# Splitting streamed weights into two rounded parts by DMA instead of by ScalarE and VectorE

## The chip, the cores and the metric

The kernel runs on one core of one Trainium2 chip. The metric is the device time of one execution in microseconds. Engines are PE (TensorE), ACT (ScalarE), DVE (VectorE), POOL (GpSimd) and SP (SyncE). A hardware profile of one execution gives the rows below.

## The reference

One layer of a hybrid decoder trunk, 512 tokens, width 1024, everything in float32:

```python
h = rmsnorm(x, g_mix[l])
u = h @ w_in[l]
c_q, c_kv, k_r, u_pool, z, xbc, dt, lru_g, lru_x, gates = jnp.split(u, pts, axis=-1)
...
gates = jax.nn.sigmoid(gates.reshape(b, s, N_BRANCH, D_MODEL))
merged = (gates[:, :, 0] * (y_a @ w_branch[l, 0])
          + gates[:, :, 1] * (y_b @ w_branch[l, 1])
          + gates[:, :, 2] * (y_c @ w_branch[l, 2])
          + gates[:, :, 3] * (y_d @ w_branch[l, 3]))
x = x + merged @ w_out[l]
h2 = rmsnorm(x, g_mlp[l])
x = x + jnp.square(jax.nn.relu(h2 @ w_ff1[l])) @ w_ff2[l]
ple_gate = jax.nn.sigmoid(rmsnorm(x, g_ple[l]) @ w_ple_gate[l])
x = x + (p[l] @ w_ple[l]) * ple_gate
```

The four branches are attention (y_a), causal pooling (y_b), a state-space mixer (y_c) and a gated linear recurrence (y_d). A final norm follows.

## The kernel before, in words

All large products run on PE in a rounded 32-bit format (float32r), with each operand split into a high part (the value rounded to that format) and a low part (the remainder). A product is three matmuls per 128 rows of depth: high by high, high by low, low by high (`mm3`, lines 208 to 210).

The weights are streamed from one tensor W in *units* of 128 partitions by up to 1024 values, 512 KB each. The list UNITS at the top of the file fixes their order. `unit(key)` (line 200) hands out a unit and loads ahead until two units beyond it are requested (LOOK = 2). `load_next` (line 165) loads one: SP's queue brings it into a raw tile (tag wr, two buffers, line 176), ACT copies it into the high part wh, which rounds it (line 177), and DVE subtracts, which gives the low part wl (line 178). wh and wl have three buffers each. Throughout this text a *pair* is one wh with its wl. The next unit takes a pair when PE has read it for the last time.

The stages that matter here, with their units:

- *Branches.* For branch n and column block j, `gate(n, j)` (line 425) multiplies a gate unit by the normed input: 8 depth blocks, 24 matmuls, and a tanh on ACT. `project(n, j)` (line 430) multiplies half a br unit by the branch's output, 12 matmuls; DVE multiplies by the gate and POOL adds to the merged sum (line 439). Branch 2 is interleaved with the projections of the recurrence (lx, lg) and of pooling (pool); branches 3 and 1 follow by themselves.
- *out.* Eight units, 24 matmuls each (line 841).
- *MLP.* Four chunks. In each, eight ff1 units of 24 matmuls (line 919), then 14 *T units* of the second matrix, which is multiplied by a Strassen-Winograd scheme of seven products (`product`, line 881). The T units use the same wh and wl buffers, filled by `right_operand` (line 185) from b tiles that SP loads (line 899) and that POOL subtracts from one another, eight operations per chunk (lines 903 and 904).

A scheduler orders each engine's instructions when the program is built, and each engine then runs its own in order. `tc.high_priority()` puts the loads forward.

Of the kernel before, what the change touches and what calls it, by code (L numbers as in the profile page):

```python
# [10 lines left out]
F32 = mybir.dt.float32  # L11
F32R = mybir.dt.float32r
I32 = mybir.dt.int32
AF = mybir.ActivationFunctionType
ALU = mybir.AluOpType
AX = mybir.AxisListType

P = 128
# [34 lines left out]
UNITS = []  # L53
UIDX = {}
# [72 lines left out]
def trunk(tc, xT, pT, pos, par_d, cst_d, gfin, wblk_d, wpool_d, W, out, dbg=None):  # L127
    nc = tc.nc
    act, dve, pool, pe, sync = nc.scalar, nc.vector, nc.gpsimd, nc.tensor, nc.sync
    TAGS = {"G1": 16, "G2": 16, "G3": 16, "T1": 6, "T2": 8, "T3": 6, "Z": 4, "X": 8}  # L130
    BANKS = {"m": 3, "s": 2, "t": 2, "o": 1}
    with ExitStack() as ctx:
        cp = ctx.enter_context(tc.tile_pool(name="cp", bufs=1))
        ap_ = ctx.enter_context(tc.tile_pool(name="ap", bufs=1))
        wp = ctx.enter_context(tc.tile_pool(name="wp", bufs=1))
# [5 lines left out]
        def nm(s):  # L141
            cnt[0] += 1
            return f"{s}_{cnt[0]}"

        def A(tag, dt=F32, n="a"):
            return ap_.tile([P, S], dt, name=nm(n), tag=tag, bufs=TAGS[tag])
# [18 lines left out]
        def load_next():  # L165
            u = state[0]
            state[0] += 1
            n = UNITS[u][1]
            if UNITS[u][0][0] == "T":
                loaded[u] = right_operand(*UNITS[u][0][1:])  # L170
                return
            with tc.high_priority():
                raw = wp.tile([P, 1024], F32, name=nm("wr"), tag="wr", bufs=2)
                hi = wp.tile([P, 1024], F32R, name=nm("wh"), tag="wh", bufs=3)
                lo = wp.tile([P, 1024], F32R, name=nm("wl"), tag="wl", bufs=3)
                sync.dma_start(out=raw[:, :n], in_=W[u, :, :n])
                act.copy(out=hi[:, :n], in_=raw[:, :n])  # L177
                dve.tensor_tensor(out=lo[:, :n], in0=raw[:, :n], in1=hi[:, :n].bitcast(F32), op=ALU.subtract)  # L178
            loaded[u] = (hi, lo)


# [3 lines left out]
        def right_operand(ch, name, v):  # L185
            hi = wp.tile([P, 1024], F32R, name=nm("wh"), tag="wh", bufs=3)
            lo = wp.tile([P, 1024], F32R, name=nm("wl"), tag="wl", bufs=3)
            with tc.high_priority():
                for u in range(2):
                    kp, c = 2 * v + u, slice(u * S, (u + 1) * S)  # L190
                    src = ff2_raw[ch, {"t2": "b11", "t3": "b12", "t4": "b21"}.get(name, name), kp]
                    act.copy(out=hi[:, c], in_=src)  # L192
                    dve.tensor_tensor(out=lo[:, c], in0=src, in1=hi[:, c].bitcast(F32), op=ALU.subtract)  # L193
                    if name == "b11":
                        dve.tensor_tensor(out=src, in0=ff2_raw[ch, "b22", kp], in1=ff2_raw[ch, "t1", kp], op=ALU.subtract)
                    elif name == "b21":
                        dve.tensor_tensor(out=src, in0=src, in1=ff2_raw[ch, "b11", kp], op=ALU.subtract)
            return hi, lo

        def unit(*key):  # L200
            u = UIDX[key]
            while state[0] <= min(u + LOOK, NRING - 1):
                load_next()
            return loaded.pop(u)
# [16 lines left out]
        def pc(name, i=0, w=1):  # L221
            o, _ = PAR[name]
            return par[:, o + i:o + i + w]
# [93 lines left out]
        for k in range(KD):  # L317
            if k:
                sync.dma_start(out=xres[k], in_=xT[:, k, :])
            if k < 3:  # L320
                load_next()
            if k == 2:
                sync.dma_start(out=cst, in_=cst_d)
            xg.append(split_scaled(xres[k], pc("gmix", k), "G1", "xg"))
            q = A("T3", F32, "sq")
            act.activation(out=q, in_=xres[k], func=AF.Square)
            if acc is None:
                acc = q
            else:
                dve.tensor_tensor(out=acc, in0=acc, in1=q, op=ALU.add)  # L330
        for k in range(KD):
            if k == 5:
                with tc.high_priority():
                    vx = SM(NT, "vx")
                    dve.tensor_scalar(out=vx, in0=token_sums(acc), scalar1=1.0 / D, scalar2=EPS,
                                      op0=ALU.mult, op1=ALU.add)
                    rxb = bcast_tokens(rsqrt(vx, NT), "T1")
            w = loaded.pop(UIDX[("lat", k)])
            for i in range(5):
                c = slice(i * P, (i + 1) * P)  # L340
                mm3(lat_ps[i], w[0][:, c], w[1][:, c], xg[k][0], xg[k][1], k == 0, k == KD - 1)
            if k + 3 < KD:
                load_next()
# [7 lines left out]
        for k in range(KD):  # L351
            n = A("T3", F32, "hn")
# [118 lines left out]
        for t in range(NT):  # L471
# [3 lines left out]
                          in1=pc("dtb", 0, 8).unsqueeze(1).to_broadcast([P, NT, 8]), op=ALU.add)  # L475
# [75 lines left out]
        for hd in range(H):  # L551
# [11 lines left out]
            for kt in range(NT):  # L563
                pt = PS("t")
                n = S - kt * P
# [22 lines left out]
            else:  # L588
# [11 lines left out]
                                 in1=ah.unsqueeze(1).to_broadcast([P, NT, 8]), op0=ALU.mult, op1=ALU.mult)  # L600
# [18 lines left out]
        def bc8(v, n=8):  # L619
            return v.unsqueeze(2).to_broadcast([v.shape[0], n, 64])  # L620
# [4 lines left out]
        def csl(c):  # L625
            return slice(c * P, (c + 1) * P)
# [19 lines left out]
        for g in range(2):  # L646
            ps = PS("s")
            gs = slice(g * 64, g * 64 + 64)
            for c in range(NT):
                pe.matmul(ps[:, csl(c)], lhsT=xbc[4][gs, csl(c)], rhs=xbc[5][gs, csl(c)], start=True, stop=True)  # L650
            dve.tensor_tensor(out=heads(cbm[g], P), in0=heads(ps, P), in1=U.unsqueeze(1).to_broadcast([P, NT, P]),
                              op=ALU.mult)
        gate(0, 6, "G1")
        for c in range(NT):
            for g in range(2):
# [4 lines left out]
                for j in range(4):  # L660
# [4 lines left out]
                                   in1=cbm[g][:, csl(c)].unsqueeze(1).to_broadcast([P, 4, P]), op=ALU.mult)  # L665
# [4 lines left out]
        for c in range(NT - 1):  # L670
# [5 lines left out]
            for g in range(2):  # L676
# [4 lines left out]
                else:  # L681
                    dve.tensor_tensor(out=heads(Rn[gs, 0:256]), in0=heads(R[c][gs, 0:256]),
                                      in1=bc8(etot[gs, c * 8 + g * 4:c * 8 + g * 4 + 4], 4), op=ALU.mult)
# [3 lines left out]
        for c in range(NT):  # L687
# [7 lines left out]
            if c > 0:  # L695
                for g in range(2):
# [5 lines left out]
                                      in1=bc8(eacs[:, c * 8 + g * 4:c * 8 + g * 4 + 4], 4), op=ALU.mult)  # L702
# [93 lines left out]
        for i in range(4):  # L796
            w = unit("pool", i)
            ps = proj(w, hh, KD)
            u = A("T3", F32, "pu")
            act.copy(out=u, in_=ps)  # L800
            src = u
            n = 1
# [148 lines left out]
        for hf in range(2):  # L951
            ws = []
            for k in range(KD):
                raw = A("T1", F32, "pgw")
# [11 lines left out]
        for hf in range(2):  # L966

            for j in range(0, KD, 2):
                ps = PS("t")
                for u in range(2):  # L970
                    for t in range(2):
                        k = j + u
                        pe.transpose(out=ps[:, (2 * u + t) * P:(2 * u + t + 1) * P],
                                     in_=xt[2 * hf + t][k // 4][:, (k % 4) * P:(k % 4 + 1) * P], identity=ident)
# [28 lines left out]
        for hf in range(2):  # L1003
            ws = pgs[hf]
            for t in range(NT):
# [6 lines left out]
                for q in range(nf):  # L1012
# [3 lines left out]
                    for k in range(KD):  # L1016
# [9 lines left out]
                                                          in1=gf[:, hf, c], op=ALU.mult)  # L1026
# [146 lines left out]
```

## Time and profile before

| | |
|---|---|
| median of 3 runs | 981.22 us (980.24 to 982.66) |
| the profiled execution | 982.21 us, its span 980.4 us |
| PE, DVE, ACT, POOL busy | 954.9, 661.4, 489.4, 138.8 us |
| mean granted clock of PE | 0.997 of full speed |
| moved by DMA | 96.95 MB, 99 GB/s |

Busy time is the union of an engine's instructions. Matmuls overlap, so their pitch is read from start to start and not from a row's duration. In a timeline row the bracket says how long the engine was idle before the instruction and what ended that. Names are tiles, out<-in, with buffer numbers left out.

### The profile page before, as it was taken

What the parts mean: (1) busy time and instruction counts of PE and PEld (TensorE: products, weight loads), DVE (VectorE), ACT (ScalarE), POOL (GpSimd) and SP (SyncE); (2) the same over time, 40 slices, a digit from 0 to 9 for tenths busy, and PEclk for the clock granted to TensorE, in tenths of its full rate; (3) what the DMA queues carried; (4) which work ended last, traced back from release to release, by engine and by line L of the source; (5) the groups of instructions that cost most, each with busy time, mean ns of one, the idle gap of its engine ahead of it and who ended that gap; (6) DMA issues with size and microseconds to landing.
All of it is one profiled execution on the core that took longest, in us unless ns stands there. A gap on an engine that the chain in (4) does not pass through costs nothing.

```text
span 980.4 us, 12002 instructions
## 1 busy us (share of the span) xinstructions
PE 954.9 (97%) x4389; PEld 782.4 (80%) x4389; DVE 661.4 (67%) x1156; ACT 489.4 (50%) x860; POOL 138.8 (14%) x107
## 2 busy tenths in 40 slices
PE   7999999999999999999999999999999999999996
PEld 5877788877777887788888888788887888887785
DVE  7768787557885753443433656996897789689636
ACT  6755777768276333222332435543543453456633
POOL 0000000005102423311122001350013005000021
PEclk9999999999999999999999999999999999999998
DMA  5423221214112332332324326134133304424002
GB/s 201 136 76 103 78 74 65 66 44 151 65 65 86 119 108 84 108 108 87 129 86 151 108 76 226 65 129 150 65 101 126 108 31 142 139 81 134 1 1 86
DMA packets 36473, 96.95 MB, mean 99 GB/s; under 512 B 4768, under 2 KB 4800, under 8 KB 36416
## 3 DMA queue, kind: packets, MB, share of 16 engines
q1 hardware_dynamic: 35472, 95.35, 29.5%
q10 hardware_dynamic: 944, 0.85, 0.3%
q8 instruction: 34, 0.56, 0.2%
q14 instruction: 23, 0.19, 0.1%
HBM read 94.01 MB, written 2.18 MB: 98 GB/s over the span
## 4 chain that ended last, share of the span: by engine, by line
PE 81%; DVE 13%; ACT 2%; issue 2%; DMA 2%; ACTq 0%; DVEq 0%
PE psm L208 21%; PE psm L210 21%; PE psm L209 21%; DVE wl L193 4%; PE pss L208 3%; PE pss L209 3%; PE pss L210 3%; DVE xtok L894 2%; DVE wl L178 1%; PE pst L567 1%; PE pst L209 1%; PE pst L208 1%; PE pso L210 1%; PE pso L208 1%; PE pso L692 1%
## 5 line engine op out<-in xcount | busy, mean ns | idle before, releaser
L177 ACT CAST wh<-wr 128x1024 fp32r<-128x1024 f32 (+3 forms) x126 | 128.7, 1023 | 227.3 <-PE psm L209 148.5
L178 DVE TENSOR_TENSOR wl<-wr,wh 128x1024 fp32r<-128x1024 f32 (+3 forms) x126 | 157.6, 1254 | 112.2 <-ACT wh L177 105.3
L208 PE MATMUL psm<-hh,wh 128*128 128x512 f32 (+1 forms) x408 | 161.5, 396 | 0.3 <-DVE rot L459 0.3
L209 PE MATMUL psm<-hl,wh 128*128 128x512 f32 (+1 forms) x408 | 161.0, 395 | 0.0
L210 PE MATMUL psm<-hh,wl 128*128 128x512 f32 (+1 forms) x408 | 159.3, 390 | 0.0
L210 PE MATMUL psm<-x2h,wl 128*128 128x512 f32 x256 | 100.0, 391 | 0.8 <-DVE wl L178 0.8
L208 PE MATMUL psm<-x2h,wh 128*128 128x512 f32 x256 | 99.9, 390 | 0.0
L209 PE MATMUL psm<-x2l,wh 128*128 128x512 f32 x256 | 99.9, 390 | 0.0
L209 PEld LDWEIGHTS psm<-hl,wh 128*128 128x128 f32 (+1 forms) x408 | 76.2, 187 | 18.4 <-issue 2.5
L208 PEld LDWEIGHTS psm<-hh,wh 128*128 128x128 f32 (+1 forms) x408 | 76.2, 187 | 18.3 <-issue 1.5
L210 PEld LDWEIGHTS psm<-hh,wl 128*128 128x128 f32 (+1 forms) x408 | 76.2, 187 | 17.3 <-issue 1.3
L193 DVE TENSOR_TENSOR wl<-b,wh 128x512 fp32r<-128x512 f32 x96 | 84.1, 922 | 1.8 <-ACT wh L192 1.6
L192 ACT CAST wh<-b 128x512 fp32r<-128x512 f32 x96 | 54.4, 618 | 56.1 <-PE pss L210 30.5
L439 POOL TENSOR_TENSOR gth<-gth,gth 128x512 f32<-128x512 f32 x24 | 36.8, 1534 | 188.4 <-DVE gth L435 188.4
L903 POOL TENSOR_TENSOR t<-b,b 128x512 f32<-128x512 f32 x16 | 25.1, 1575 | 239.9 <-DVE xtok L894 163.7
L210 PEld LDWEIGHTS psm<-x2h,wl 128*128 128x128 f32 x256 | 48.1, 188 | 11.5 <-DVE wl L178 1.7
L209 PEld LDWEIGHTS psm<-x2l,wh 128*128 128x128 f32 x256 | 48.1, 188 | 9.9
L208 PEld LDWEIGHTS psm<-x2h,wh 128*128 128x128 f32 x256 | 48.1, 188 | 9.8
L921 DVE SCALAR_TENSOR_TENSOR ffr<-psm,bc 128x512 f32<-128x512 f32 x32 | 21.8, 688 | 33.9 <-PE psm L210 30.6
L638 POOL TENSOR_TENSOR xsd<-xt,par 128x512 f32<-128x512 f32 x4 | 5.5, 1392 | 224.5 <-ACT xt L634 224.5
L435 DVE SCALAR_TENSOR_TENSOR gth<-gth,psm 128x512 f32<-128x512 f32 x32 | 21.9, 685 | 14.9 <-PE psm L210 14.8
L1025 POOL TENSOR_TENSOR xtok<-xtok,gf 128x512 f32<-128x512 f32 x7 | 9.0, 1289 | 134.4 <-ACT pth L1024 134.4
(398 smaller groups left out, 2084.9 us busy)
## 6 DMA issues: line engine op xcount, KB each, us to landing
wr<-W SPq DMA_DIRECT2D x114, 512.0 KB, 3.3
b<-W SPq DMA_DIRECT2D x64, 256.0 KB, 3.4
pgw<-W SPq DMA_DIRECT2D x16, 256.0 KB, 2.9
x<-xT SPq DMA_DIRECT2D x15, 256.0 KB, 5.2
wr<-W SPq DMA_DIRECT2D x8, 320.0 KB, 3.6
E<-acd SPq DMA_DIRECT2D x8, 256.0 KB, 4.4
out<-xtok SPq DMA_DIRECT2D x8, 256.0 KB, 2.1
wr<-W SPq DMA_DIRECT2D x3, 384.0 KB, 2.9
```

The source lines that it names most:

```text
L177: act.copy(out=hi[:, :n], in_=raw[:, :n])
L178: dve.tensor_tensor(out=lo[:, :n], in0=raw[:, :n], in1=hi[:, :n].bitcast(F32), op=ALU.subtract)
L192: act.copy(out=hi[:, c], in_=src)
L193: dve.tensor_tensor(out=lo[:, c], in0=src, in1=hi[:, c].bitcast(F32), op=ALU.subtract)
L208: pe.matmul(ps, lhsT=s_h, rhs=m_h, start=first, stop=False, **kw)
L209: pe.matmul(ps, lhsT=s_h, rhs=m_l, start=False, stop=False, **kw)
L210: pe.matmul(ps, lhsT=s_l, rhs=m_h, start=False, stop=last, **kw)
L435: dve.scalar_tensor_tensor(out=th, in0=th, scalar=1.0, in1=pb, op0=ALU.add, op1=ALU.mult)
L439: pool.tensor_tensor(out=merged[j], in0=merged[j], in1=th, op=ALU.add)
L894: dve.tensor_tensor(out=xt[t0 + t][hf], in0=xt[t0 + t][hf], in1=banks[t], op=ALU.add)
L903: pool.tensor_tensor(out=t1, in0=b12, in1=b11, op=ALU.subtract)
L921: dve.scalar_tensor_tensor(out=r, in0=ps, scalar=0.0, in1=rb, op0=ALU.max, op1=ALU.mult)
```

## The change

Units of four kinds (gate, br, out, ff1) that come after the first br unit are no longer loaded by SP into a raw tile. POOL's queue transfers them from W straight into wh, which is float32r, so that the transfer converts. ACT writes the negative of wh into wl. A second transfer from W on POOL's queue adds to wl. The units are 3 br units of branch 0, 12 units of branch 2, 24 of branches 3 and 1, 8 of out and 32 of ff1: 79 of the 126 that are loaded. The others keep the raw tile.

```diff
             with tc.high_priority():
-                raw = wp.tile([P, 1024], F32, name=nm("wr"), tag="wr", bufs=2)
                 hi = wp.tile([P, 1024], F32R, name=nm("wh"), tag="wh", bufs=3)
                 lo = wp.tile([P, 1024], F32R, name=nm("wl"), tag="wl", bufs=3)
-                sync.dma_start(out=raw[:, :n], in_=W[u, :, :n])
-                act.copy(out=hi[:, :n], in_=raw[:, :n])
-                dve.tensor_tensor(out=lo[:, :n], in0=raw[:, :n], in1=hi[:, :n].bitcast(F32), op=ALU.subtract)
+                if UNITS[u][0][0] in ("gate", "br", "out", "ff1") and u > UIDX["br", 0, 0]:
+
+                    pool.dma_start(out=hi[:, :n], in_=W[u, :, :n])
+                    act.activation(out=lo[:, :n], in_=hi[:, :n].bitcast(F32), func=AF.Copy, scale=-1.0)
+                    pool.dma_start(out=lo[:, :n], in_=W[u, :, :n], accum_op=ALU.add)
+                else:
+                    raw = wp.tile([P, 1024], F32, name=nm("wr"), tag="wr", bufs=2)
+                    sync.dma_start(out=raw[:, :n], in_=W[u, :, :n])
+                    act.copy(out=hi[:, :n], in_=raw[:, :n])
+                    dve.tensor_tensor(out=lo[:, :n], in0=raw[:, :n], in1=hi[:, :n].bitcast(F32), op=ALU.subtract)
             loaded[u] = (hi, lo)
```

Lines after the edit stand six further down than before (L439 becomes L445).

The scheduler sets the new instructions into the old order. The first place is POOL's queue in branch 3 (gth is the merged sum). Before:

```order
L439 TENSOR_TENSOR gth_2106<-gth_2106,gth_3939 128x512
L439 TENSOR_TENSOR gth_2141<-gth_2141,gth_3987 128x512
L439 TENSOR_TENSOR gth_2261<-gth_2261,gth_4041 128x512
L439 TENSOR_TENSOR gth_2314<-gth_2314,gth_4089 128x512
L439 TENSOR_TENSOR gth_2411<-gth_2411,gth_4143 128x512
```

After (wh and wl with DMA are the first and the second transfer; wh_3933 and wh_3965 are gate units, wh_3985 is a br unit):

```order
L177 DMA wh_3933<-W 128x1024
L445 TENSOR_TENSOR gth_2106<-gth_2106,gth_3916 128x512
L177 DMA wh_3965<-W 128x1024
L179 DMA wl_3934<-W 128x1024
L445 TENSOR_TENSOR gth_2141<-gth_2141,gth_3963 128x512
L179 DMA wl_3966<-W 128x1024
L177 DMA wh_3985<-W 128x1024
L179 DMA wl_3986<-W 128x1024
L177 DMA wh_4032<-W 128x1024
```

Of three units, two first transfers now stand ahead of a second one, and the merge adds stand between them.

The second place is POOL's queue before the last chunk of the MLP (b are blocks of the second matrix, t their differences). Before, the eight subtractions were followed by the kernel's end:

```order
L904 TENSOR_TENSOR b_1493_7142<-b_1494_7144,b_1493_7142 128x512
L903 TENSOR_TENSOR t_1517_7244<-b_1515_7240,b_1513_7236 128x512
L903 TENSOR_TENSOR t_1541_7344<-b_1539_7340,b_1537_7336 128x512
L904 TENSOR_TENSOR b_1515_7240<-b_1516_7242,b_1515_7240 128x512
L904 TENSOR_TENSOR b_1539_7340<-b_1540_7342,b_1539_7340 128x512
L1025 TENSOR_TENSOR xtok_5059<-xtok_5059,gf 128x512
```

After:

```order
L910 TENSOR_TENSOR b_1418_7067<-b_1419_7069,b_1418_7067 128x512
L909 TENSOR_TENSOR t_1440_7167<-b_1438_7163,b_1436_7159 128x512
L909 TENSOR_TENSOR t_1462_7265<-b_1460_7261,b_1458_7257 128x512
L910 TENSOR_TENSOR b_1438_7163<-b_1439_7165,b_1438_7163 128x512
L910 TENSOR_TENSOR b_1460_7261<-b_1461_7263,b_1460_7261 128x512
L177 DMA wh_6927<-W 128x1024
L177 DMA wh_6944<-W 128x1024
L179 DMA wl_6928<-W 128x1024
L177 DMA wh_6976<-W 128x1024
L179 DMA wl_6945<-W 128x1024
L179 DMA wl_6977<-W 128x1024
```

The transfers of the chunk's first ff1 units follow the subtractions.

The third place is PE where the second chunk's ff1 begins (q2 belongs to the last T unit, x2 is the normed residual). Before:

```order
L208 MATMUL pss_5411<-wh_5626,q2h_5393 128x512
L209 MATMUL pss_5411<-wl_5627,q2h_5393 128x512
L210 MATMUL pss_5411<-wh_5626,q2l_5394 128x512
L208 MATMUL psm_5703<-x2h_4872,wh_5647 128x512
L209 MATMUL psm_5703<-x2l_4873,wh_5647 128x512
L210 MATMUL psm_5703<-x2h_4872,wl_5648 128x512
L208 MATMUL psm_5703<-x2h_4876,wh_5647 128x512
L209 MATMUL psm_5703<-x2l_4877,wh_5647 128x512
```

After:

```order
L214 MATMUL pss_5356<-wh_5571,q2h_5338 128x512
L215 MATMUL pss_5356<-wl_5572,q2h_5338 128x512
L216 MATMUL pss_5356<-wh_5571,q2l_5339 128x512
L214 MATMUL psm_5645<-x2h_4823,wh_5591 128x512
L215 MATMUL psm_5645<-x2l_4824,wh_5591 128x512
L214 MATMUL psm_5678<-x2h_4823,wh_5608 128x512
L215 MATMUL psm_5678<-x2l_4824,wh_5608 128x512
L216 MATMUL psm_5645<-x2h_4823,wl_5592 128x512
L214 MATMUL psm_5645<-x2h_4827,wh_5591 128x512
L215 MATMUL psm_5645<-x2l_4828,wh_5591 128x512
```

Two matmuls of the second ff1 unit (wh_5608) now stand ahead of the first use of a low part (wl_5592). In the branches PE's order changed alike: two matmuls of a gate come before the second half of the product ahead of it, two of the next gate after that half, and the 22 others of each gate follow.

## Rows read from the trace of the kernel before

**Rows 1.** The page: span, and busy us (share of the span) xinstructions by engine.

```profile
span 980.4 us, 12002 instructions
...
PE 954.9 (97%) x4389; PEld 782.4 (80%) x4389; DVE 661.4 (67%) x1156; ACT 489.4 (50%) x860; POOL 138.8 (14%) x107
```

**Rows 2.** PE's waits from 300 to 900 us: who for, us in total, times, longest.

```profile
PE pss L208 <- DVE xtok L894: 1.1, 3, 0.5
PE psm L210 <- DVE wl L178: 0.8, 2, 0.4
PE pst L209 <- DVE wl L193: 0.7, 1, 0.7
PE pss L208 <- ACT wh L192: 0.2, 1, 0.2
```

**Rows 3.** PE's timeline in branch 3 (start us, us, engine line op, tiles, shapes).

```profile
408.61 0.39 PE L208 MATMUL psm<-hh,wh 128*128 128x512 f32 x1
...
414.05 0.39 PE L208 MATMUL psm<-ydh,wh 128*128 128x512 f32 x1
...
416.77 0.39 PE L208 MATMUL psm<-hh,wh 128*128 128x512 f32 x1
```

**Rows 4.** ACT's and DVE's timelines in the same branch.

```profile
430.34 1.05 ACT L177 CAST wh<-wr 128x1024 fp32r<-128x1024 f32 x1 [6.62 <-PE psm L209]
...
431.43 1.23 DVE L178 TENSOR_TENSOR wl<-wr,wh 128x1024 fp32r<-128x1024 f32 x1 [5.54 <-ACT wh L177]
433.36 0.69 DVE L435 SCALAR_TENSOR_TENSOR gth<-gth,psm 128x512 f32<-128x512 f32 x1 [0.70 <-PE psm L210]
```

**Rows 5.** SP's longest wait, and its issues at line 176 (ns min/median/max).

```profile
SPq L176 <- DVE wl L178: 499.4, 101, 11.0
...
L176 SPq DMA_DIRECT2D wr<-W x126: 327/328/424, 1.2 to 858.7; - x126
```

**Rows 6.** DMA by queue and by issue (count, KB each, median us to landing).

```profile
q1 hardware_dynamic: 35472, 95.35, 29.5%
...
wr<-W SPq DMA_DIRECT2D x114, 512.0 KB, 3.3
...
x<-xT SPq DMA_DIRECT2D x15, 256.0 KB, 5.2
...
cst<-cst_d SPq DMA_DIRECT2D x1, 418.5 KB, 6.6
```

**Rows 7.** POOL's timeline in branch 3.

```profile
425.96 1.28 POOL L439 TENSOR_TENSOR gth<-gth,gth 128x512 f32<-128x512 f32 x1 [6.88 <-DVE gth L435]
```

**Rows 8.** POOL's timeline before the last chunk of ff1.

```profile
813.11 1.29 POOL L903 TENSOR_TENSOR t<-b,b 128x512 f32<-128x512 f32 x1 [69.49 <-DVE xtok L894]
...
819.46 3.53 POOL L903 TENSOR_TENSOR t<-b,b 128x512 f32<-128x512 f32 x2
822.96 3.44 POOL L904 TENSOR_TENSOR b<-b,b 128x512 f32<-128x512 f32 x2
```

**Rows 9.** ACT's timeline there.

```profile
820.34 1.14 ACT L192 CAST wh<-b 128x512 fp32r<-128x512 f32 x2 [1.12 <-PE pst L210]
823.06 1.06 ACT L177 CAST wh<-wr 128x1024 fp32r<-128x1024 f32 x1 [1.58 <-PE pst L210]
```

**Rows 10.** PE's timeline there.

```profile
822.63 0.39 PE L210 MATMUL pst<-wh,q4l 128*128 128x512 f32 x1
822.86 0.62 PE L208 MATMUL pss<-wh,q2h 128*128 128x512 f32 x2
...
828.09 0.39 PE L210 MATMUL pss<-wh,q2l 128*128 128x512 f32 x1
828.32 0.39 PE L208 MATMUL psm<-x2h,wh 128*128 128x512 f32 x1
...
829.33 0.50 PE L210 MATMUL psm<-x2h,wl 128*128 128x512 f32 x1 [0.40 <-DVE wl L178]
```

**Rows 11.** Stretches of 50 us, the last columns PE clock, DMA share, GB/s.

```profile
400.00:450.00 50.00, 50.00 (x220) 41.05 (x219) 19.39 (x17) 13.14 (x17) 7.71 (x6) 1.00 0.32 106
...
550.00:600.00 50.00, 50.00 (x238) 41.82 (x238) 27.84 (x48) 19.65 (x29) 0.00 (x0) 1.00 0.39 131
```

## The prediction

> **What bounds the kernel now.** The page's busy times come first: TensorE (PE) is busy 954.9 of 980.4 us, and no other engine passes 67% [rows 1]. So only work on PE, or a wait of PE, can move the end. The second view is PE's waits from 300 to 900 us, the stretch of most edited units: four causes, 2.8 us together [rows 2]. That is all that faster loading could give back there. The third is PE's timeline in the branches: one gate (24 matmuls) begins at 408.61 and the next product at 414.05, so a unit takes 5.44 us; half a br unit, from 414.05 to 416.77, takes 2.72 [rows 3]. The pitch is 0.227 us, although a matmul's own row says 0.39. Last, how a weight tile comes free. ACT's cast into wh waits for PE (6.62 us) and takes 1.05; DVE's subtraction starts 0.04 us after it and takes 1.23 [rows 4]. The raw tile was loaded long before, since SP sits 499.4 us waiting only for DVE to finish with a raw tile [rows 5]. So after PE lets a wh/wl pair go, 2.3 us pass until the pair is full again. With three pairs, PE needs it 10.9 us later (two units of 5.44): that is why loading is hidden.
>
> **What the change does to that chain.** It takes 79 subtractions off DVE (79 x 1.23 = 97 us of work [rows 4]), and 79 loads off SP, whose issue takes 0.33 us each [rows 5]. Both engines are off the path, so I cost this at nothing; what hides it is PE. ACT's work stays: one pass of the same 128x1024 shape, which I take at the 1.05 of the cast. What counts is that the raw tile was also the early copy. Now nothing can be fetched before PE releases the pair, and the refill is transfer, ACT pass, transfer, in a row.
>
> Refill time L, piece by piece:
> - *First transfer, h.* The nearest row is the same 512 KB from W by SP's queue, 3.3 us from issue to landing [rows 6]. The trace has no transfer issued by POOL. POOL writes them by work of its own, for which the nearest row is one POOL operation, 1.28 us [rows 7]. I take 3.3 + 1.3 = 4.6. Bounds: 3.3 (no dearer than SP's) and 6.6 + 1.3 = 7.9, from the slowest of the large loads, cst [rows 6].
> - *ACT, a.* 1.05 and 0.1 for the handover on either side (0.04 seen): 1.25.
> - *Second transfer, l.* It also reads what it adds to, one pass more. The hardware queue moved 95.35 MB in 29.5% of 980.4 us [rows 6], so 330 GB/s, and 512 KB (0.524 MB) is a pass of 1.6 us. So l = 4.6 + 1.6 = 6.2; bounds 3.3 (the third pass overlaps) and 7.9 + 1.6 = 9.5.
> - *Sharing.* First and second transfers of neighbouring units now overlap on the same engines: 0.5, between nothing and one pass of 1.6.
>
> L = 4.6 + 1.25 + 6.2 + 0.5 = 12.6 us, against the 2.3 of before; the bounds give 7.9 and (with the full pass of sharing) 20.3. Beyond 10.9 it cannot be hidden.
>
> The row of SP's load [rows 6] gave 4.6 for the first transfer. The Trainium skill, page "DMA: Bandwidth & Descriptors", section "Latency and other measured facts", has the first byte of a GpSimd-issued transfer only 0.4 us later than that of a SyncE- or ScalarE-issued one (about 1 against 0.6). By that figure h would be 3.7 and l 5.3, L 10.8 (an estimate), the chunk starts 24 us, the rest 13, and the total about 1019 instead of 1060. No run here shows it yet.
>
> **Where the excess falls.** Each term is L against the room.
> - *Branches 3 and 1, 24 units, 8 turns of three pairs.* In the new order a br pair is released after its second half, and that half plus the first and four early matmuls of the next gates take 5.9 us of the turn; a turn lasts max(16.3, L + 5.9) = 18.5. Excess 2.2 x 8 = 17.6 us. POOL's own order adds nothing at this L: the low part of one gate stands behind the high part of the next, which waits for the next release, but that is 5 us and the first transfer with ACT takes 5.9 anyway. The merged add (1.28 us) in the same queue fits in between.
> - *out and the first eight ff1, 16 units, 5.3 turns* of L + 5.4 = 18.0: 1.7 x 5.3 = 9.
> - *Branch 2, 12 units among 12 others that SP still loads.* Those others need 2.3 us only, but POOL's queue mixes the DMAs with pooling, gelu and merge operations that wait for DVE and ACT. Per br pair, one low part stands behind an add that waits for the product: product, then 0.7 DVE [rows 4], 1.3 POOL, 6.2 + 0.5 of transfer make 8.7 against a unit of 5.4. So 3.3, about 3 after rounding down for the other work on PE, x 4 = 12; at the upper bound of l, 6 x 4 = 24.
> - *br units of branch 0 (3):* state-space work on PE lies between; nothing.
> - *Start of ff1 in chunks 1, 2, 3.* Here PE is at its least patient. Before, the pair for the first ff1 unit is free at about 822.9, ACT casts at 823.06, and PE reaches ff1 at 828.32, waiting 0.40 [rows 9, 10]. In the new POOL queue the first DMA stands behind the eight subtractions of the next chunk's blocks, which began at 813.11 and end at 826.4 [rows 8]. So the pair fills at 826.4 + 12.6 = 839.0, and PE, which can do four early matmuls, wants it at 829.2: 9.8 us. The next two pairs are requested meanwhile; the fourth unit and those after it lack 1.7 and some 1.5 more. 13 us per chunk, 39 in all.
>
> Behind the waiting ACT pass stand gate tanhs and ff1 squares, which wait for PE anyway; three psum banks cover them. Behind a waiting DMA on POOL stand merge adds, whose readers come a branch later. SP reaches the b blocks sooner, which are bound by their tiles' release, not by the queue: nothing.
>
> Sum: 17.6 + 9 + 12 + 39 = 78 us. The profiled execution took 982.2 us, for a span of 980.4 [rows 1]; 982.2 + 78 = 1060. It is 1 us above the median of 981.2, which is less than the 0.3% (2.9 us) that a measurement of this kernel tells from no change. At the lower bound only the chunk starts remain: 826.4 + 7.9 - 829.2 = 5.1, three times, 15 us: 997. Near the upper bound, at L = 18.7 (without sharing), the terms are 8 x 8.3, 5.3 x 7.8, 24 and 3 x 31 = 225: 1207.
>
> **Rivals.**
> 1. *The adding transfer is bound by rate, not by latency.* Per unit the engines carry one pass of 1.6 us for the first transfer and two for the second; if the adding one runs at half rate its two take 6.4, and the unit 8.0 us for 5.44 of PE. Then 79 x (8.0 - 5.44) = 202 us, 1184. For it: nothing in this trace adds in a transfer. Against: the engines' share in these stretches is 0.32 to 0.39 [rows 11], so two to three times the bytes still fit. Decides where the two transfers of a unit take more than 5.44 us of the engines.
> 2. *Transfers no dearer than SP's* (L = 7.9): 997. For it: the same bytes, the same engines. Against: two in a row, one of them reading twice.
> 3. *Not slower.* The eight subtractions ahead of the first ff1 DMA end sooner, because DVE has 97 us less to do and they wait first for DVE [rows 8], and the refill stays under 6.3 us (822.9 to 829.2). Then no term is left and the 2.8 us of waits [rows 2] fall: 979. Against: the DVE operations in that stretch are splits of T units, which the change leaves alone, and 6.3 us is less than two of the 3.3 us landings.
> If the transfers rounded nothing the time would be as forecast: the same bytes move.
>
> **How the numbers follow.** Forecast (L between 10 and 19): 0.71. Rival 1: 0.13; rival 2: 0.07; rival 3: 0.05; slower than all of these, by descriptors cut small or a queue that stalls more than I see: 0.04. The time is the forecast's, 1060. The range, 995 to 1225, takes in rival 2 and the forecast up to L near 19, and most of rival 1. Of rival 3's 0.05, 0.03 is within 0.3% (979 is 2.2 us under the median) and 0.02, with some stall gone that I don't see, faster by more. Slower: 0.95.
>
> **What would show it.** PE's idle time should move to waits for DMA into wl, from 0 to about 75 us, most per unit at the first ff1 of chunks 1 to 3 (some 10 us each), and 2 us in every third unit of the branches. Landing of the loads on POOL's queue should read 4 to 5 us for wh and 6 to 7 for wl. DVE should be near 565 us busy, SP's waits for wl gone. Wrong: wl landing under 5 us with PE at 97% still (rival 2 or 3), a DMA share above 0.9 in the branches (rival 1), or waits on POOL's adds rather than on transfers.

## The result and the profile after

The changed kernel takes 1107.2 us (median of four runs, 1100.1 to 1112.8) where the kernel before takes 981.3: a ratio of 1.128, with a 95% interval of 1.125 to 1.130. Forecast were 1060 us, in a range of 995 to 1225. The direction and the mechanism held; 47 us of the 126 were not in the sum, and the profile tells which.

The page of the changed kernel, its span and busy times, to be laid beside [rows 1]:

```profile
span 1105.5 us, 12091 instructions
...
PE 997.0 (90%) x4389; PEld 794.5 (72%) x4389; DVE 560.8 (51%) x1077; ACT 491.4 (44%) x860; POOL 244.9 (22%) x265
```

The span grew by 125.1 us. PE executes the same 4389 matmuls, yet the growth has two parts: PE's idle time (span less busy) went from 25.5 to 108.5, which is 83.0 more, and its *busy* time went from 954.9 to 997.0, 42.1 more. DVE lost 100.6 us of work, as forecast, and it bought nothing.

PE's two longest waits in the changed kernel (what for, us in total, times, longest), where before there were 2.8 us for all causes from 300 to 900 us [rows 2]:

```profile
PE psm L216 <- DMA wl<-W: 64.3, 35, 4.4
PE psm L214 <- DMA wh<-W: 11.1, 5, 3.6
```

So 75.4 us of waits stand against transfers of POOL's queue, most of it for the low part, the last link of the refill. The same run's DMA view (queues: packets, MB, share of 16 engines; issues: count, KB each, median us to landing), beside [rows 6]:

```profile
q0 software_dynamic: 22752, 82.85, 33.5%
...
wh<-W POOLq DMA_DIRECT2D x79, 512.0 KB, 4.9
wl<-W POOLq DMA_DIRECT2D x79, 512.0 KB, 5.5
```

Where the time went is read from the windows of the two kernels, cut at PE's first matmul of each stage: branch 2, branches 3 and 1, out, the first eight ff1, and from the first T unit to the last. (Columns: stretch, length, busy us of PE, PE's weight loads, DVE, ACT and POOL with their counts, then PE's granted clock, DMA share, GB/s.) Before:

```profile
283.10:405.90 122.80, 122.80 (x531) 98.61 (x530) 67.84 (x82) 55.82 (x78) 38.00 (x36) 1.00 0.30 98
405.90:531.00 125.10, 125.10 (x553) 103.57 (x552) 48.56 (x46) 36.58 (x48) 22.43 (x15) 1.00 0.31 102
531.00:574.50 43.50, 43.50 (x193) 36.04 (x192) 24.07 (x30) 17.15 (x23) 2.33 (x1) 1.00 0.39 132
574.50:623.60 49.10, 49.10 (x242) 41.16 (x241) 32.52 (x53) 21.67 (x36) 11.57 (x8) 1.00 0.46 152
623.60:913.20 289.60, 286.02 (x1257) 234.30 (x1255) 243.27 (x371) 143.49 (x243) 38.92 (x24) 1.00 0.32 103
```

After (and three short stretches of branch 3, read further down):

```profile
285.20:418.20 133.00, 124.48 (x507) 97.60 (x505) 52.44 (x70) 57.14 (x79) 52.02 (x60) 0.95 0.52 131
418.20:572.60 154.40, 134.14 (x555) 104.97 (x556) 16.13 (x25) 36.87 (x46) 53.16 (x62) 0.98 0.71 160
572.60:633.10 60.50, 47.82 (x193) 37.72 (x192) 13.74 (x21) 16.66 (x22) 13.79 (x19) 0.94 0.77 186
633.10:691.10 58.00, 51.68 (x242) 41.83 (x241) 20.13 (x42) 23.92 (x38) 15.85 (x19) 0.97 0.72 179
691.10:1038.20 347.10, 308.89 (x1280) 243.42 (x1278) 222.38 (x356) 144.62 (x245) 77.37 (x76) 0.95 0.49 124
...
420.00:424.00 4.00, 3.68 (x10) 2.96 (x11) 0.00 (x0) 0.00 (x0) 0.24 (x1) 0.64 0.96 250
440.00:444.00 4.00, 1.84 (x4) 1.49 (x5) 0.00 (x0) 0.00 (x0) 1.74 (x2) 0.70 0.92 173
456.00:460.00 4.00, 2.96 (x13) 2.47 (x14) 0.00 (x0) 0.00 (x0) 0.00 (x1) 1.00 0.99 211
```

Length less PE's busy time is its idle time. That gives, in us:

| stage | idle, more than before | forecast | busy, more than before |
|---|---|---|---|
| branch 2 | 8.5 | 12 | 1.7 |
| branches 3 and 1 | 20.3 | 17.6 | 9.0 |
| out and the first eight ff1 | 19.0 | 9 | 6.9 |
| T units and ff1 of chunks 1 to 3 | 34.6 | 39 | 22.9 |
| sum | 82.4 | 78 | 40.5 |

The forecast was a sum of waits, and as that it came out: 82.4 against 78. Part of this is luck, for the terms missed by 3.5 too much, 2.7 too little, 10 too little and 4.4 too much, which largely cancel. The busy column is what the forecast left out.

How a wait comes about is seen in POOL's timeline in branch 3, where one turn of three pairs goes from the first transfer at 463.32 to that at 483.03, 19.7 us (forecast 18.5, before 16.3):

```profile
463.32 0.87 POOL L177 DMA_DIRECT2D wh<-W  x1
...
467.39 0.59 POOL L177 DMA_DIRECT2D wh<-W  x1 [1.88 <-PE psm L216]
471.37 0.88 POOL L179 DMA_DIRECT2D wl<-W  x1 [3.39 <-ACT wl L178]
...
474.70 0.55 POOL L177 DMA_DIRECT2D wh<-W  x1 [0.22 <-PE psm L216]
482.49 0.85 POOL L179 DMA_DIRECT2D wl<-W  x1 [7.23 <-ACT wl L178]
483.03 0.87 POOL L177 DMA_DIRECT2D wh<-W  x1
```

ACT's pass for the unit of 474.70, and PE's waits for the low part of the unit of 463.32 and then of 483.03, which use the same pair one turn apart:

```profile
481.13 1.06 ACT L178 ACTIVATE wl<-wh 128x1024 fp32r<-128x1024 f32 x1 [7.99 <-DMA wh<-W]
...
476.81 0.50 PE L216 MATMUL psm<-hh,wl 128*128 128x512 f32 x1 [1.74 <-DMA wl<-W]
...
495.94 0.50 PE L216 MATMUL psm<-hh,wl 128*128 128x512 f32 x1 [1.62 <-DMA wl<-W]
```

POOL waits in turn for PE to release a wh and for ACT's pass, which itself waits for the first transfer. The unit asked for at 474.70 gets its second transfer only at 482.49: its first one landed after 6.4 us, since it ran beside an adding transfer of the unit before. And the request of 483.03 stands in POOL's queue behind that second transfer, about 0.8 us after PE left the pair it fills (482.2). Over all 79 units, the time from the first issue to the landing of the second transfer has a median of 13.0 us (10.1 to 17.5, from POOL's timeline and the landings). The forecast L was 12.6.

In branch 2 one wait has another cause. The request for a high part stands behind four multiplications that POOL does for the recurrence:

```profile
318.25 6.41 POOL L770 TENSOR_TENSOR xc<-xc,m 128x512 f32<-128x512 f32 x4 [1.43 <-ACT m L768]
324.62 0.60 POOL L177 DMA_DIRECT2D wh<-W  x1
...
330.05 0.76 PE L214 MATMUL psm<-hh,wh 128*128 128x512 f32 x1 [3.57 <-DMA wh<-W]
```

It returns, as 4.5 and 4.4 us, in two of the kernels below that have no serial refill.

PE's timeline in branch 3 shows what a wait does beyond its own length:

```profile
442.16 0.80 PE L216 MATMUL psm<-hh,wl 128*128 128x512 f32 x1 [3.15 <-DMA wl<-W]
442.75 0.63 PE L214 MATMUL psm<-hh,wh 128*128 128x512 f32 x1
443.18 0.63 PE L215 MATMUL psm<-hl,wh 128*128 128x512 f32 x1
...
445.17 0.39 PE L214 MATMUL psm<-hh,wh 128*128 128x512 f32 x1
445.40 0.39 PE L215 MATMUL psm<-hl,wh 128*128 128x512 f32 x1
```

After the wait the matmuls follow each other at 0.43 us (442.75 to 443.18) where they otherwise do at 0.23 (445.17 to 445.40). The granted clock in the window 440 to 444 above is 0.70, in 420 to 424, behind a wait of 1.35 us, it is 0.64: PE spends part of these stretches at 1.2 instead of 2.4 GHz. Not each wait does it, and its own length does not decide: the window 456 to 460 holds the end of a wait of 1.96 us and reads 1.00. Over the whole run PE's timeline has 117 matmuls at that slow pitch (0.41 to 0.45 us), 30 before. All matmuls in stretches of lowered clock together took 24 us more than they would at 0.227: that is the clock's share of the 42. Another 10 us lie at the edges of 52 more gaps, 0.2 us each, since the last matmul before a gap ends without a successor on top. Of the remaining 8, about half lie in the first two matmuls behind a wait, which follow at up to 0.34 us; the rest stays open.

### The profile page after: what moved, and what is told of

The parts are those of the page before. It is cut to its first block, busy times and chain, and to the rows that moved or that the text cites. A ratio compares the mean times of both kernels' runs of the same rounds, so it can differ in the third digit from the quotient of the medians.

```text
span 1105.5 us, 12091 instructions
## 1 busy us (share of the span) xinstructions
PE 997.0 (90%) x4389; PEld 794.5 (72%) x4389; DVE 560.8 (51%) x1077; ACT 491.4 (44%) x860; POOL 244.9 (22%) x265
## 3 DMA queue, kind: packets, MB, share of 16 engines
q0 software_dynamic: 22752, 82.85, 33.5%
q1 hardware_dynamic: 24096, 53.93, 14.9%
## 5 line engine op out<-in xcount | busy, mean ns | idle before, releaser
L178 ACT ACTIVATE wl<-wh 128x1024 fp32r<-128x1024 f32 x79 | 83.7, 1060 | 295.1 <-DMA wh<-W 238.3
L216 PE MATMUL psm<-hh,wl 128*128 128x512 f32 (+1 forms) x408 | 162.5, 401 | 21.4 <-DMA wl<-W 21.3
L216 PE MATMUL psm<-x2h,wl 128*128 128x512 f32 x256 | 104.8, 414 | 27.0 <-DMA wl<-W 27.0
L177 POOL DMA_DIRECT2D wh<-W x79 | 52.4, 664 | 336.0 <-PE psm L216 334.2
L179 POOL DMA_DIRECT2D wl<-W x79 | 69.7, 882 | 256.4 <-ACT wl L178 220.4
L214 PE MATMUL psm<-x2h,wh 128*128 128x512 f32 x256 | 105.7, 414 | 7.7 <-DMA wh<-W 7.5
L216 PEld LDWEIGHTS psm<-hh,wl 128*128 128x128 f32 (+1 forms) x408 | 77.6, 190 | 44.1 <-DMA wl<-W 27.1
L215 PE MATMUL psm<-x2l,wh 128*128 128x512 f32 x256 | 104.5, 409 | 0.0
L184 DVE TENSOR_TENSOR wl<-wr,wh 128x1024 fp32r<-128x1024 f32 (+3 forms) x47 | 52.9, 1127 | 30.8 <-ACT wh L183 30.2
L214 PEld LDWEIGHTS psm<-x2h,wh 128*128 128x128 f32 x256 | 51.0, 199 | 20.9 <-DMA wh<-W 10.9
L183 ACT CAST wh<-wr 128x1024 fp32r<-128x1024 f32 (+3 forms) x47 | 45.6, 973 | 42.3 <-PE psm L215 23.0
L215 PEld LDWEIGHTS psm<-x2l,wh 128*128 128x128 f32 x256 | 51.1, 200 | 10.8
L909 POOL TENSOR_TENSOR t<-b,b 128x512 f32<-128x512 f32 x16 | 25.1, 1594 | 92.8 <-DVE xtok L900 61.9
```

Source lines behind the costliest of these rows:

```text
L177: pool.dma_start(out=hi[:, :n], in_=W[u, :, :n])
L178: act.activation(out=lo[:, :n], in_=hi[:, :n].bitcast(F32), func=AF.Copy, scale=-1.0)
L179: pool.dma_start(out=lo[:, :n], in_=W[u, :, :n], accum_op=ALU.add)
L214: pe.matmul(ps, lhsT=s_h, rhs=m_h, start=first, stop=False, **kw)
L215: pe.matmul(ps, lhsT=s_h, rhs=m_l, start=False, stop=False, **kw)
L216: pe.matmul(ps, lhsT=s_l, rhs=m_h, start=False, stop=last, **kw)
```

## Experiments

Nine kernels. Theory A is that of the prediction: the refill is a serial chain that starts only when PE releases a pair, and the adding transfer makes it long. Its rivals are the bytes moved, POOL's queue order, and, for PE's busy time, another cause than the waits.

**Four high parts.** A fourth wh (wl stays at three), loads one unit further ahead, and one raw tile instead of two to make room:

```diff
-        LOOK = 2
+        LOOK = 3
-                hi = wp.tile([P, 1024], F32R, name=nm("wh"), tag="wh", bufs=3)
+                hi = wp.tile([P, 1024], F32R, name=nm("wh"), tag="wh", bufs=4)
-                    raw = wp.tile([P, 1024], F32, name=nm("wr"), tag="wr", bufs=2)
+                    raw = wp.tile([P, 1024], F32, name=nm("wr"), tag="wr", bufs=1)
```

> High parts get a fourth buffer (with one raw tile instead of two, which pays for it), and three units are requested ahead; low parts keep three. Theory A (a refill of two transfers in a row, longer than the room that three pairs leave): now only the ACT pass and the adding transfer, 1.06 + 5.5 = 6.6 us, follow the release of a low part, less than the 10.9 of room, so branches 3 and 1 go from 154 us back to about 127, out from 60 to about 45, and the run ends at 1020 to 1050. Theory B (the transfers are bound by the DMA engines' rate): the same bytes move, so branches 3 and 1 stay above 145 us and the run stays above 1090.

Measured: 1056.4 us, ratio 1.076 (1.073 to 1.079). 51 us came back, and out fell to 45.4 us, nearly its 43.5 of before. The total is 6 us above theory A's band, and the branches stayed at 144.1, between the two theories. The start got slower: the first product of branch 0 stands at 233.4 instead of 206.8. I put this down to the single raw tile, since PE waits 15.0 us for ACT's casts there, 6.9 in the changed kernel; no run tests it. The windows of branches 3 and 1 and of out:

```profile
430.00:574.10 144.10, 130.69 (x553) 105.02 (x552) 15.92 (x23) 36.88 (x47) 51.94 (x61) 0.98 0.78 172
574.10:619.50 45.40, 43.87 (x194) 35.97 (x194) 15.06 (x22) 16.94 (x23) 12.55 (x17) 1.00 1.03 257
```

In out the DMA share reads 1.03, the time of the packets adds up to all of the engines', and PE still waits only 1.5 us. Why the branches did not come back is taken up by the last experiment.

**Both transfers at once.** No ACT pass; the second transfer is a plain one. The low part is not computed.

```diff
-                    act.activation(out=lo[:, :n], in_=hi[:, :n].bitcast(F32), func=AF.Copy, scale=-1.0)
-                    pool.dma_start(out=lo[:, :n], in_=W[u, :, :n], accum_op=ALU.add)
+                    pool.dma_start(out=lo[:, :n], in_=W[u, :, :n])
```

> The ACT pass is gone and the second transfer is a plain one like the first, so the low part is not computed (wl holds W). Both transfers of a unit can go at once. Theory A: refill about 5 to 6 us, hidden in the branches; only the chunk starts remain, 2 to 3 us each; 985 to 1000 us and a granted clock above 0.985. Theory B (rate): 79 units still move twice, without the read-back; the branches stay 15 us or more longer than before and the run ends above 1030.

Measured: 1006.6 us, 1.025 (1.023 to 1.027). Branches 3 and 1 take 125.2 us and out 43.5, as before the change, with the same bytes read from memory on the same queue. So in the branches and in out the bytes and POOL's queue are hidden. Elsewhere the queue is not: the total is 6.6 above the band, since the chunk starts still cost 16.6 us (5.5 each, not 2 to 3) and branch 2 takes 129.9 us instead of 122.8. POOL's own arithmetic still stands ahead of requests there, and PE waits 14.9 us for wh, 10.4 of them at the chunk starts and 4.5 in branch 2.

**The chain without the adding.** ACT's pass stays and the second transfer overwrites what it wrote. The low part is not computed.

```diff
-                    pool.dma_start(out=lo[:, :n], in_=W[u, :, :n], accum_op=ALU.add)
+                    pool.dma_start(out=lo[:, :n], in_=W[u, :, :n])
```

> Everything as in the changed kernel, but the second transfer overwrites wl instead of adding to it, so the low part is not computed. This takes away the adding alone. Theory A: the refill gets shorter by what adding costs in landing, 5.5 to about 4.9 us, some 0.6 us; at about 30 us of time per us of refill, 1107 falls to 1080 to 1095. Theory B (the adding is what is dear): landing of wl falls well below 5 us and the run below 1050.

Measured: 1043.3 us, 1.062 (1.058 to 1.066). Theory A's band was missed and its rival's met: I had held the adding for a small part of the chain, and it is half of the loss. The DMA view, against that of the changed kernel:

```profile
q0 software_dynamic: 22752, 82.85, 25.1%
...
wh<-W POOLq DMA_DIRECT2D x79, 512.0 KB, 4.4
wl<-W POOLq DMA_DIRECT2D x79, 512.0 KB, 3.8
```

The second transfer lands in 3.8 us instead of 5.5, the first in 4.4 instead of 4.9. The refill's median falls from 13.0 to 9.8 us, below the room of 10.9, and the branches take 128.8 us. Engine time follows from the shares: 25.1% of 1043.1 us is 262 us for 158 plain transfers, 1.66 each; 33.5% of 1105.5 is 370, less 79 x 1.66, if the plain ones take the same there, leaves 3.03 for an adding one. (The five of each that ran with nothing else in flight in the changed kernel took 1.78 and 3.15.) Yet out still takes 55.7 us, though 9.8 is below 10.9. There PE's order holds the last depth block of the first out unit back to the end of the second, because its input, the last merged block, comes last. So two pairs come free together, and the next two refills run into one another. The changed kernel shows the same: the additions that read the first two products start at 595.2 and 595.8, and POOL's timeline has one group of two issues at 595.26 ("x2") after a wait for PE of 7.72 us. The room was smaller there than I had counted.

**First three ff1 units of chunks 1 to 3 the old way.**

```diff
-                if UNITS[u][0][0] in ("gate", "br", "out", "ff1") and u > UIDX["br", 0, 0]:
+                if (UNITS[u][0][0] in ("gate", "br", "out", "ff1") and u > UIDX["br", 0, 0]
+                        and UNITS[u][0] not in [("ff1", c * 8 + o) for c in (1, 2, 3) for o in (0, 4, 1)]):
```

> The first three ff1 units of chunks 1, 2 and 3 (nine units) are loaded the old way, by SP, ACT and DVE. Theory A: the waits at the chunk starts (6.7 us in the last chunk's first unit) go, and the stretch from the first T unit to the last goes from 347 us to 315 to 325; the run ends at 1072 to 1085. Rival (the loss in the chunks is spread over all ff1 units, or is the clock's): less than 10 us are gained.

Measured: 1076.3 us, 1.097 (1.090 to 1.103). In the profiled execution, which took 1069.5 us and was the fastest of the four, the stretch of T units took 319.1 us, inside the band. So the nine units at the chunk starts cost about 28 of the 57.5 us lost there. The other units lose the rest.

**Subtractions on DVE.** The eight per chunk leave POOL's queue.

```diff
-            pool.tensor_tensor(out=t1, in0=b12, in1=b11, op=ALU.subtract)
-            pool.tensor_tensor(out=b12, in0=b22, in1=b12, op=ALU.subtract)
+            dve.tensor_tensor(out=t1, in0=b12, in1=b11, op=ALU.subtract)
+            dve.tensor_tensor(out=b12, in0=b22, in1=b12, op=ALU.subtract)
```

> The eight subtractions per chunk that stand ahead of the first ff1 transfers in POOL's queue are done by DVE instead. Theory (the queue's order costs about 3 us at each chunk start): the first ff1 transfer goes when its pair is released, and the stretch from the first T unit to the last, 347 us, gets 7 to 12 us shorter; the run ends at 1094 to 1101. Rival (the pair's release is what comes last there): within 4 us of 1107.

Measured: 1085.7 us, 1.108 (1.105 to 1.111), 8 us below the band; the T stretch fell by 13.3 us, a little more than the 7 to 12 expected, and the rest of the gain lies ahead of it and is not explained. What the queue held up is seen in POOL's timeline at the last chunk. The changed kernel, then this one:

```profile
929.08 3.44 POOL L910 TENSOR_TENSOR b<-b,b 128x512 f32<-128x512 f32 x2
932.46 1.16 POOL L177 DMA_DIRECT2D wh<-W  x2
938.01 0.88 POOL L179 DMA_DIRECT2D wl<-W  x1 [4.39 <-ACT wl L178]
```

```profile
914.83 0.55 POOL L177 DMA_DIRECT2D wh<-W  x1 [41.04 <-PE pst L216]
917.55 0.54 POOL L177 DMA_DIRECT2D wh<-W  x1 [2.17 <-PE pss L216]
920.13 0.89 POOL L179 DMA_DIRECT2D wl<-W  x1 [2.04 <-ACT wl L178]
```

In the first, two requests go out together behind the last subtraction. In the second, each goes when PE releases its wh. In the changed kernel PE then pays at the first unit of that chunk:

```profile
933.75 0.39 PE L216 MATMUL pss<-wh,q2l 128*128 128x512 f32 x1
936.59 0.80 PE L214 MATMUL psm<-x2h,wh 128*128 128x512 f32 x1 [2.46 <-DMA wh<-W]
...
943.34 0.79 PE L216 MATMUL psm<-x2h,wl 128*128 128x512 f32 x1 [4.26 <-DMA wl<-W]
```

2.46 and 4.26 make 6.7 us; 9.8 were forecast.

**Only the high part by POOL.** The low part the old way, from a raw tile that SP loads.

```diff
-                    act.activation(out=lo[:, :n], in_=hi[:, :n].bitcast(F32), func=AF.Copy, scale=-1.0)
-                    pool.dma_start(out=lo[:, :n], in_=W[u, :, :n], accum_op=ALU.add)
+                    raw = wp.tile([P, 1024], F32, name=nm("wr"), tag="wr", bufs=2)
+                    sync.dma_start(out=raw[:, :n], in_=W[u, :, :n])
+                    dve.tensor_tensor(out=lo[:, :n], in0=raw[:, :n], in1=hi[:, :n].bitcast(F32), op=ALU.subtract)
```

> The first transfer rounds into wh as in the changed kernel, but the low part is made as before: SP loads a raw tile ahead and DVE subtracts. The ACT pass and the adding are gone; both parts are computed and the same bytes come from memory as in the changed kernel. Theory A (a serial refill against the room): refill 4 to 5 + 1.23 us, under 10.9, so the branches are as before and only the chunk starts lose 2 to 4 us each; 985 to 998. Rival (any refill by POOL's queue stalls, by its order or its issue): above 1015.

Measured: 1001.3 us, 1.022 (1.019 to 1.024), 3 us above the band. Branches 3 and 1 take 125.1 us, out 44.1. With the early copy back, the branches hide a first transfer of 4.1 us; what stays is at the chunk starts and in branch 2. This is the fastest of the kernels that load through POOL's queue, and still 2% behind the kernel before.

**More work for PE inside the wait.** Three extra matmuls per product that need only the high part, 258 in all; the next matmul overwrites what they give.

```diff
+                if k == 0 and fill:
+                    for _ in range(fill):
+                        pe.matmul(ps[:m, :], lhsT=w[0][:, c], rhs=acts[0][0], start=True, stop=True)
```

> The changed kernel with 258 matmuls more on PE, three ahead of a gate, out or ff1 unit's products and of each br unit's first half; each needs only the high part, and its result is overwritten by the product that follows. At 0.227 us they are 58 us of work, put where PE waits for low parts. Clock theory (PE's clock falls because PE waits): the granted clock rises from 0.967 to 0.985 or more, and the run stays between 1085 and 1115. Rival (the clock falls for another reason, or the waits do not take the fill): clock 0.96 to 0.975 and 1120 to 1165.

Measured: 1130.0 us, 1.153 (1.150 to 1.155), clock 0.979. The time lies in the rival's band and the clock between the two expectations, so by itself the run settled nothing about the clock. The page adds up all the same: 258 x 0.227 = 58.6 us of work raised PE's busy time by only 45.8 (1042.8 against 997.0), and the idle time fell from 108.5 to 85.9. So 22.6 us of the work went into waits, 12.8 of slow matmuls came back, and 23.2 were paid.

**Waits without the transfers.** The question that stood open was whether PE's waits lower its clock, or the transfers do. The kernel before, with five more identical ACT copies per unit:

```diff
                 act.copy(out=hi[:, :n], in_=raw[:, :n])
+                if UNITS[u][0][0] in ("gate", "br", "out", "ff1") and u > UIDX["br", 0, 0]:
+                    for _ in range(5):
+                        act.copy(out=hi[:, :n], in_=raw[:, :n])
```

> The kernel before, all loads by SP, with five extra identical ACT copies of the raw tile into wh for each of the 79 units (same output). ACT then needs about 6 x 1.05 = 6.3 us per unit and some 0.6 of its own work where PE needs 5.44, so PE waits for ACT, some 1 to 1.5 us a unit, 80 to 120 us in all, with the traffic of the kernel before and nothing on POOL's queue. Theory (PE's waits are what brings the granted clock down): mean clock 0.96 to 0.985, stretches of PE below 0.9 in the branches, PE busy 20 us or more above the 955 of before. Rival (the transfers of POOL's queue bring it down): mean clock 0.99 or more, PE busy within 10 us of before, and the time is that of before and the waits alone.

Measured: 1144.5 us, 1.166 (1.164 to 1.168), clock 0.955, a little under the theory's band. The page of that kernel (busy times, and the queue of its loads), and then PE's two longest waits:

```profile
PE 1015.3 (89%) x4389; PEld 804.6 (70%) x4389; DVE 659.0 (58%) x1156; ACT 871.4 (76%) x1255; POOL 133.6 (12%) x107
...
q1 hardware_dynamic: 35472, 95.35, 25.0%
```

```profile
PE psm L211 <- ACT wh L180: 79.8, 32, 8.6
PE psm L213 <- DVE wl L181: 11.4, 19, 1.5
```

Nothing is on POOL's queue, the bytes are those of before, and PE is 60.4 us busier than before. A wait in branch 3 shows the slow stretch behind it, first in PE's timeline, then in a window (clock 0.58):

```profile
446.52 0.50 PE L211 MATMUL psm<-hh,wh 128*128 128x512 f32 x1 [2.96 <-ACT wh L180]
...
448.31 0.63 PE L212 MATMUL psm<-ydl,wh 128*128 128x512 f32 x1
448.74 0.63 PE L213 MATMUL psm<-ydh,wl 128*128 128x512 f32 x1
```

```profile
447.00:451.00 4.00, 4.00 (x13) 3.09 (x12) 0.72 (x1) 3.87 (x5) 0.00 (x0) 0.58 0.41 131
```

The rival falls as the only cause: waits for ACT alone bring the clock down. The next run shows that the transfers without waits do not.

**Four high parts, without the adding.** The first kernel of this section with the overwriting second transfer. The low part is not computed.

```diff
-                    pool.dma_start(out=lo[:, :n], in_=W[u, :, :n], accum_op=ALU.add)
+                    pool.dma_start(out=lo[:, :n], in_=W[u, :, :n])
```

> Four pairs as in the run with four, and the second transfer overwrites wl instead of adding (the low part is not computed). Theory A (with four pairs the branches stayed slow because the adding transfers load the engines and slow their neighbours): branches 3 and 1 in 125 to 132 us against 144 with the adding transfer, total 1015 to 1035. Theory B (the order of POOL's queue, a transfer standing behind one that waits for a release, holds them whatever the transfer costs): branches 3 and 1 above 138 us, total above 1040.

Measured: 1032.1 us, 1.052 (1.050 to 1.054). The branches' window:

```profile
428.10:553.20 125.10, 125.10 (x553) 103.59 (x552) 15.92 (x23) 36.82 (x47) 44.13 (x61) 1.00 0.65 196
```

125.1 us, with no idle time, against 144.1 with the adding. POOL's queue order is the same in both, so it is the adding that held the branches with four high parts: its own landing (6.4 against 4.6 us) and what it takes from the engines (their share 0.78 against 0.65); which of the two weighs more stays open. The granted clock of this stretch is 1.00, with POOL's transfers at work and no wait of PE.

## Why the prediction was right, and where it was not

- **The mechanism held.** The early copy was gone, and the refill became a serial chain of 13.0 us in the median (12.6 forecast) against a room of 10.9. PE's waits for POOL's transfers are 75.4 us ("about 75"), and PE's idle time grew by 83.0 (78). Taking the chain apart with the bytes kept brought the branches back to 125 us, in two ways; shortening it to 9.8 brought them to 128.8. The sizes of the single terms are another matter, as the next points say.
- **The step that fell short is the sum itself, "982.2 + 78 = 1060".** It priced a wait at its own length and let PE run at its pitch of 0.227 us between waits. PE was 42.1 us busier for the same matmuls, 24 us of it in stretches of lowered clock and 10 at the edges of the gaps. The run with ACT copies shows that waits do this without any new transfer. In the changed kernel and the nine of the experiments, against before (the 58.6 us of extra matmuls taken off where there are any), the busy time grew by 0.5 to 0.8 us for each us of idle time: 42.1 for 83.0 here, 60.4 for 100.9 with the ACT copies, 9.2 for 12.0 with only the high part. Had I multiplied the 78 by 1.5, the forecast would have been 1099.
- **"Out and the first eight ff1: 9" was mis-sized: 19.0 idle.** I took a room of two units and one L everywhere. In out PE lets two pairs go at once, and the 16 refills of this stretch took a median of 14.3 us, where the 24 of branches 3 and 1 took 13.0. With 14.3 the prediction's own term, (14.3 + 5.4 - 16.3) x 5.3, would have been 18.0.
- **"Branches 3 and 1: 17.6"** measured 20.3 of idle time; the turn shown was 19.7 us where 18.5 were forecast. The prediction let the br pair set the turn and took POOL's order for nothing. In the turn shown PE's longest wait is at the first gate behind it: 5.4 us of use, 0.8 until its request comes up behind a second transfer, and 12.9 of refill make the 19.1 from 476.81 to 495.94. (The 5.9 in the prediction is two halves and two early matmuls, 26 of 0.227 us; its words say four.)
- **"Branch 2: 12"** measured 8.5, and not as told. Low parts cost 4.7 us in three waits, and 3.6 went to the one high part behind POOL's four multiplications, which had no term.
- **"13 us per chunk, 39"** measured 34.6. PE waits 6.7 us for the first ff1 unit of the last chunk instead of 9.8. Its refill is shorter than L there, from 932.46 to 943.34 is 10.9 us, and the four early matmuls, which run at the slow pitch, take up some of the wait. The order of POOL's queue, subtractions first, was right, as moving them off showed.
- **Pieces of L: near in sum, by two errors that cancel.** The five first transfers that ran with nothing else in flight landed in 3.55 to 3.75 us (SP's of the same run, alone, in a median of 3.2), so 4.6 was too much. The 51 of the 79 that overlapped an adding transfer by 2 us or more landed in a median of 6.2, so "sharing 0.5" was far too little. The median of all is 4.9. The second transfer took 5.5 (6.2), ACT's pass 1.06 (1.05). That 12.6 comes so near 13.0 is in part luck.
- **The figure of the Trainium skill,** "DMA: Bandwidth & Descriptors", section "Latency and other measured facts", would have made L 10.8 and the total 1019. Its 0.4 us between the two kinds of issue agrees with the transfers that ran alone (3.56 against 3.2), better than the 1.3 of the prediction. What that sum lacks is what the adding transfers do to the ones beside them; the refill takes 13.0.
- **Rivals.** Rival 1 (the adding is bound by rate) was half there: an adding transfer does take 3.03 us of all engines, nearly twice a plain one's 1.66, but a unit's two make 4.7, below the 5.44 from which it would decide, and the DMA share in the branches is 0.71, not above 0.9. Rival 2 was right on a first transfer alone (3.56) and falls by the rest: the refill is 13.0, not 7.9. Rival 3 falls: the subtractions ended 1.3 us before PE's last matmul of the chunk (932.46 and 933.75), where before it was 1.7 (826.40 and 828.09), and no refill stayed under 6.3 us.
- **Nothing for DVE and SP** fits: DVE lost 100.6 us of work, and nothing in PE's waits shows a gain from it. No run takes this apart.

The Trainium skill, "Collectives: The Full Stack", section "The bandwidth ceiling: the fold count and why AG ≠ RS ≠ AR", says of ReduceScatter that it is slower than AllGather because the add needs two source reads, not because adding costs. The ratio here, 3.03 to 1.66, is consistent with two reads; no run here separates the reading from the adding.

## What to carry to other kernels

A staging tile that looks like one copy too many may be what lets a load start before its consumer lets go of the last buffer; count the refill from release to full, against the room until the buffer is wanted, before removing it. Where the bounding engine is TensorE, price a us of new waiting above its own length: here it cost 1.5 to 1.8 us, largely because the clock fell with it. Count what the new transfers do to one another, not only what one takes alone. Read the room per stage from the order in which buffers are really released, and look at what stands ahead of a request in its queue.

## What the runs showed of the hardware

- PE's granted clock fell in and behind waits of 1.35 to 3.15 us (0.58 to 0.70 in the windows shown, matmuls at 0.43 instead of 0.227 us), for a transfer and for ACT alike, but not behind one of 1.96 us. In the changed kernel each of the twelve stretches of lowered clock before the end of the work begins in or behind a wait, of 1.35 to 4.43 us; without a wait the clock stayed at 1.00 beside the same queue's transfers (the last run, branches 3 and 1). The Trainium skill's page "TensorE: Matmul & The Clock Gate", section "HAM oscillation — how this bites in real kernels", tells of a kernel whose waits for DMA bring TensorE down to half its clock. These rows agree, and the run with ACT copies shows it for waits on an engine.
- An adding transfer of 512 KB took 3.03 us of the 16 engines and landed in 5.5 us, a plain one on the same queue 1.66 and 3.8 (medians of the changed kernel and of the one without the adding). Its issue held POOL for 0.88 us, that of a plain one for 0.53 to 0.59 in the median, but 0.87 right behind an adding one (483.03).
- A first transfer of POOL's queue landed in 3.56 us with nothing else in flight and in 6.2 beside an adding one (medians of the changed kernel).
